# Six pairs of gate units per layer multiplied in seven quarter products (Strassen), placed behind the attention

## The chip, the cores and the metric

The kernel runs on one core of one Trainium2 chip. Five engines work side by side, each through its own queue of instructions: TensorE (PE) multiplies, VectorE (DVE), ScalarE (ACT) and GpSimd (POOL) compute on vectors, and SyncE (SP) issues the transfers. The metric is the time of one execution on the device in microseconds (us), the median of several runs.

## The reference, cut to what matters

Two layers of a decoder trunk with three attention branches a, b, c for 512 tokens and a model width of 1024. The part that the change touches is the merge. In short:

```
h = rmsnorm(x, norm_g[layer])                       # (512, 1024)
u = h @ w_in[layer]                                 # q, k, v, z of every branch, and ga, gb, gc: 3 x 1024 gate columns
ya, yb, yc = attention branches, each * silu(z)     # widths 256, 384, 384
merged = sigmoid(ga) * (ya @ w_br_a) + sigmoid(gb) * (yb @ w_br_b) + sigmoid(gc) * (yc @ w_br_c)
x = x + merged @ w_out[layer]
```

After the second layer a final RMSNorm follows. All is float32.

## The kernel before, in words

**Precision.** A float32 product is made of three matmuls in the type fp32r. Each operand is split into a high part (a cast to fp32r) and a low part (what the cast left); `mm3` (L125) adds high x high, high x low and low x high in PSUM.

**Tiling.** Everything is transposed: columns of a weight lie on the 128 partitions of the result and tokens run along its free dimension. A *unit* is 128 output columns for all 512 tokens: 8 k tiles of 128 input rows x 3 terms = 24 matmuls of 512 columns (`run_unit`, L133). The operands of the x side, XH[k] and XL[k], are x times norm_g, split, without the root of the mean square; that root, `rbc`, is multiplied in afterwards, at eviction.

**Weights.** They lie packed in `wpk` in the order of use, 256 KB per half a unit. `dma_to` (L880) issues their transfers on SP into five buffers called `raw`; `split_to` (L898) casts each on ACT (L905, `wh`) and subtracts on DVE (L907, `wl`). A ring of six such pairs, RING, runs ahead of PE.

**The M items.** `m_item(l, br, i)` (L570) makes one of the 24 gate units of a layer with its branch product: the unit (24 matmuls), then the product of the branch's result Y with its weights `p` (2 or 3 k tiles, 6 or 9 matmuls). What follows: L586 on DVE multiplies the gate by rbc out of PSUM, L587 on ACT takes tanh, L596 (L593 for branch 0) on DVE forms (tanh + 1) x product, and the result is added to the merge tile `mg`: by POOL for branch 1 (L598), by DVE for branch 2 (L600). After branch 2 the merge tile is complete and is split again: L605 on ACT casts, L606 on DVE subtracts. These split tiles, MH and ML, feed the output projection (`o_item`, L615, and in the last layer `last_projection`, which works in halves of 256 tokens).

**The order.** PE runs its instructions in the order in which the list `items` is written. That order is a hand-made plan: during the attention, 16 heads follow each other through scores, transposition and the product with v, and a dictionary `plan` puts projections (qa, kb, zc ...) and M items between them, so that PE has work while softmax runs on the other engines. There M(0,0..7) and M(1,0..7) are placed; M(2,0..7) follow behind the attention, one after another. On DVE, ACT and POOL the order comes from the Tile scheduler, which sorts by program order and priority; `urgent` (L111) raises the priority of what it wraps. PSUM has eight banks: three for units and branch products (`mm`), four for the attention (`att`), one `pv`. At the end of layer 1, from the last M item on, `manual_schedule` fixes the written order on all engines.

## Time and profile before

| | |
|---|---|
| time, median of 3 runs | 892.59 us (892.52 to 892.83) |
| the profiled execution | 892.23 us, of which the span of the core is 890.4 us |
| busy: PE | 879.3 us (99%), 4434 matmuls |
| busy: DVE | 607.4 us (68%), 1280 instructions |
| busy: ACT | 463.7 us (52%), 964 instructions |
| busy: POOL | 127.4 us (14%), 98 instructions |
| clock granted to PE | full (2.4 GHz) in all but the last of 40 slices, which shows 0.8 |
| transfers | 89.26 MB, mean 100 GB/s |

How to read it: busy time is an engine's own work within the span; several engines are busy at once. A matmul's duration is that of one instruction in a pipeline, so the time between two starts tells more than the duration of one. In time: the heads of layer 0 with their fillers run from about 60 to 338 us, M(2,0..7) from there to 399, then the output projection and the first projections of layer 1. In layer 1 the heads end at about 771 us and the last M item at 836; the last projection in halves closes the span.

### The profile page before, as it was taken

The numbers are of one execution on the slowest core, as the hardware profiler recorded it, in microseconds if no ns is written. First come the engines' busy times: TensorE is split into PE (matmuls) and PEld (weight loads), VectorE is DVE, ScalarE is ACT, GpSimd is POOL, SyncE is SP. The second block draws the span as 40 slices with busy tenths as digits, with TensorE's granted clock in tenths as the row PEclk, the third lists the DMA queues.
The fourth block names the chain that finished last, engine by engine and source line by source line (L and its number), as shares of the span: only waits on it lengthen the run. The fifth ranks groups of instructions, "written<-read, shape, count | busy, mean of one in ns | idle before, by whom it ended". The sixth has DMA issues, their size and how long they took to land.

```text
span 890.4 us, 13001 instructions
## 1 busy us (share of the span) xinstructions
PE 879.3 (99%) x4434; PEld 739.4 (83%) x4434; DVE 607.4 (68%) x1280; ACT 463.7 (52%) x964; POOL 127.4 (14%) x98
## 2 busy tenths in 40 slices
PE   9999999999999999999999999999999999999996
PEld 6988888888888888888889888888888888888895
DVE  7668899998765646554446879999886655555433
ACT  7467566665554434433335856666554544333542
POOL 5000231210001110001110012212100111100531
PEclk9999999999999999999999999999999999999998
DMA  6632322323232323335532332233222232233423
GB/s 216 187 96 71 107 72 89 113 69 94 73 98 82 95 84 105 95 98 167 149 134 84 85 86 85 77 101 101 83 84 76 87 89 86 77 98 94 129 78 113
DMA packets 53875, 89.26 MB, mean 100 GB/s; under 512 B 7344, under 2 KB 15920, under 8 KB 53808
## 3 DMA queue, kind: packets, MB, share of 16 engines
q1 hardware_dynamic: 53664, 88.42, 32.9%
q8 instruction: 35, 0.57, 0.3%
q14 instruction: 32, 0.26, 0.1%
q10 hardware_dynamic: 144, 0.01, 0.0%
HBM read 78.96 MB, written 4.19 MB: 93 GB/s over the span
## 4 chain that ended last, share of the span: by engine, by line
PE 96%; DVE 1%; issue 1%; DMA 1%; ACT 0%; SPq 0%; DVEq 0%; ACTq 0%
PE mm L127 26%; PE mm L128 26%; PE mm L126 26%; PE pv L545 4%; PE att L499 3%; PE att L435 2%; PE att L434 2%; PE att L230 1%; PE att L231 1%; PE att L229 1%; PE mm L256 1%; PE mm L257 1%; PE mm L258 1%; DMA mg<-in_xT_dram 1%; DVE xl L155 0%
## 5 line engine op out<-in xcount | busy, mean ns | idle before, releaser
L126 PE MATMUL mm<-xh,wh 128*128 128x512 f32 x736 | 293.1, 398 | 0.0
L905 ACT CAST wh<-raw 128x512 fp32r<-128x512 f32 (+3 forms) x277 | 163.4, 593 | 247.7 <-PE mm L127 191.7
L128 PE MATMUL mm<-xh,wl 128*128 128x512 f32 x736 | 290.5, 395 | 0.0
L127 PE MATMUL mm<-xl,wh 128*128 128x512 f32 x736 | 290.3, 394 | 0.0
L907 DVE TENSOR_TENSOR wl<-raw,wh 128x512 fp32r<-128x512 f32 (+3 forms) x272 | 182.4, 672 | 68.1 <-ACT wh L905 67.2
L128 PEld LDWEIGHTS mm<-xh,wl 128*128 128x128 f32 x736 | 138.2, 188 | 32.5
L127 PEld LDWEIGHTS mm<-xl,wh 128*128 128x128 f32 x736 | 138.4, 188 | 30.6
L126 PEld LDWEIGHTS mm<-xh,wh 128*128 128x128 f32 x736 | 138.4, 188 | 30.5
L470 ACT ACTIVATE P<-P,ng 128x256 f32<-128x256 f32 (+3 forms) x128 | 67.0, 525 | 38.0 <-DVE ng L468 38.0
L586 DVE TENSOR_TENSOR tmp<-mm,rbc 128x512 f32<-128x512 f32 x48 | 33.2, 691 | 55.9 <-PE mm L128 55.9
L345 POOL TENSOR_TENSOR tmp<-tmp,cos 128x512 f32<-128x512 f32 x20 | 31.4, 1568 | 257.8 <-DVE tmp L337 241.1
L127 PE MATMUL mm<-y,wh 128*128 128x512 f32 (+1 forms) x156 | 60.0, 384 | 0.3 <-DVE y L606 0.3
L126 PE MATMUL mm<-y,wh 128*128 128x512 f32 (+1 forms) x156 | 60.0, 384 | 0.0
L128 PE MATMUL mm<-y,wl 128*128 128x512 f32 (+1 forms) x156 | 60.0, 384 | 0.0
L598 POOL TENSOR_TENSOR mg<-mg,tmp 128x512 f32<-128x512 f32 x16 | 25.8, 1611 | 235.7 <-DVE tmp L596 235.7
L525 DVE TENSOR_TENSOR PL<-att,PH 128x512 fp32r<-128x512 f32 (+2 forms) x84 | 46.6, 600 | 0.2
L587 ACT ACTIVATE tmp<-tmp 128x512 f32<-128x512 f32 x48 | 30.4, 634 | 22.9 <-DVE tmp L586 22.8
L596 DVE SCALAR_TENSOR_TENSOR tmp<-tmp,mm 128x512 f32<-128x512 f32 x32 | 22.0, 688 | 28.5 <-PE mm L128 27.4
L524 ACT CAST PH<-att 128x512 fp32r<-128x512 f32 (+2 forms) x84 | 39.5, 526 | 2.4 <-PE att L499 1.2
L488 DVE TENSOR_SCALAR P<-P,den 128x256 f32<-128x256 f32 (+3 forms) x128 | 38.4, 364 | 1.1
L435 PE MATMUL att<-qk,qk 128*128 128x256 f32 (+2 forms) x128 | 37.1, 309 | 0.0
L499 PEld LDWEIGHTS att<-ident,P 128*128 128x128 f32 x284 | 32.9, 141 | 4.1
(197 smaller groups left out, 1374.5 us busy)
## 6 DMA issues: line engine op xcount, KB each, us to landing
raw<-in_wpk_dram SPq DMA_DIRECT2D x232, 256.0 KB, 2.6
raw<-in_wpk_dram SPq DMA_DIRECT2D x32, 192.0 KB, 2.3
tmp<-tmp SPq DMA_DIRECT2D x80, 64.0 KB, 2.0
raw<-in_wpk_dram SPq DMA_DIRECT2D x8, 260.0 KB, 2.8
mg<-in_xT_dram SPq DMA_DIRECT2D x8, 256.0 KB, 5.7
raw<-in_wpk_dram SPq DMA_DIRECT2D x16, 128.0 KB, 2.0
sz<-in_xT_dram SPq DMA_DIRECT2D x8, 256.0 KB, 3.0
x1d<-tmp SPq DMA_DIRECT2D x8, 256.0 KB, 3.3
```

The lines of the kernel that those rows point to most:

```text
L126: nc.tensor.matmul(ps, wh, xh, start=first, stop=False)
L127: nc.tensor.matmul(ps, wh, xl, start=False, stop=False)
L128: nc.tensor.matmul(ps, wl, xh, start=False, stop=last)
L435: nc.tensor.matmul(ps, q2[:, qs], k2[:, a:a + n], start=False, stop=True)
L470: nc.scalar.activation(pb, pb, AF.Exp, bias=ng[:, i:i + 1], scale=-1.0, accum_out=den[:, i:i + 1])
L488: nc.vector.tensor_scalar(blks[i], blks[i], den[:, i:i + 1], None, op0=ALU.mult)
L499: nc.tensor.transpose(ps[:, c * P:(c + 1) * P], pt[:, src * P:(src + 1) * P], st["ident"])
L524: nc.scalar.copy(hh, bk[:, :n])
L525: nc.vector.tensor_tensor(st["PL"][:, o:o + n], bk[:, :n], rd(hh), op=ALU.subtract)
L545: nc.tensor.matmul(ps[:, q:q + n], v[j], src[:, o:o + n], start=w == 0 and m == 0, stop=w == 1 and m == 3)
L905: (nc.vector.tensor_copy if i == 0 else nc.scalar.copy)(h[:, :w], r[:, :w])
L907: eng.tensor_tensor(lo[:, :w], r[:, :w], rd(h[:, :w]), op=ALU.subtract)
```

## The change

**What it does.** Per layer, M(0,0..7) and M(1,0..3) stay as they are. The other twelve M items become six pairs, (1,4), (1,6), (2,0), (2,2), (2,4) and (2,6): a pair is two neighbouring gate units, so 256 columns of a weight with 1024 rows, times 1024 x 512 of x. `pair_steps` multiplies each with Strassen's scheme in the form with seven products: weights and x are cut in 2 x 2 quarters, so a product multiplies 4 k tiles of 128 rows and 128 columns of weights with 256 tokens: 4 x 3 terms = 12 matmuls of 256 columns, and the seven take 84. Two M items took 2 x 24 = 48 matmuls of 512 columns for the same gates. The branch products of the pair stay (2 x 9 matmuls of 512 columns).

**Combinations of weights.** They are formed in place in the `raw` tiles before the split: form 2 on DVE (L1101), form 3 in two subtractions (L1103, L1104) and form 5 (L1106) on POOL. The four blocks B11, B12, B22, B21 of a pair are loaded ahead, and the `p` weights of pairs come through the two `sz` buffers.

**Combinations of x.** `sums(l, k)` forms once per layer, for each of the 4 k tiles, the four combinations that products 2 to 5 read: it loads the two x tiles, scales them on ACT, takes two halves on POOL and two on DVE (L601, L603), casts on ACT and subtracts the low part on DVE (L608). sums(3) is placed in the last head, sums(2), (0), (1) behind the attention, ahead of M(1,2) and M(1,3). The results lie in tiles that the attention no longer uses.

**Behind the products.** The seven products go into three PSUM banks a, b, c from the attention's pool, some added to what stands there. Evictions e1 (ACT, L728), c11 (DVE, L731), e5 (ACT, L735), e2 (ACT, L738), c12 (L741), c22 (L744) and c21 (L749, all DVE) bring the quarters together; L693 multiplies by rbc, L699 takes tanh, L706 forms the merge and L707 adds it on POOL for every pair but the last (2,6), where DVE adds. L718 and L719 split the finished merge of branch 2. All steps of branch 2 are `urgent`.

**Order.** The heads' slots b11 to b16 lose seven M items; M(1,2) and M(1,3) follow the attention, then the pairs. The output projection reads the k tiles in the order LATE, 7 before 6. The loader has new rules for when a buffer may be filled (`dma`).

In lines of the new kernel mm3 is at L127 to L129, the weights' transfer L1078, cast L1116 and subtraction L1118, M items' L629 (times rbc), L636 and L639 (merge), L641 (POOL's addition).

```diff
-MS = 7
+LATE = (0, 1, 2, 3, 4, 5, 7, 6)
...
+    def sum_places(k):
+        if k < 2:
+            return tuple(T([P, 8, P], F32R, f"vb{2 * k + w}").rearrange("p h d -> p (h d)") for w in range(2))
+        if k == 2:
+            return st["PH"][:, P:P + 1024], st["PL"][:, P:P + 1024]
+        return tuple(T([P, 1280], F32R, "P", 2)[:, :1024] for _ in range(2))
+
+    def sums_x(l, k):
+
+        src = xT if l == 0 else x1d
+        d = []
+        for kk in (k, k + 4):
+            t = tmp()
+            nc.sync.dma_start(t, src[:, kk, :])
+            nc.scalar.activation(t, t, AF.Copy, scale=g_sb[:, l, kk:kk + 1])
+            d.append(t)
+        return d
+
+    def sums(l, k):
+        def run():
+            a, b = sums_x(l, k)
+            u, v = tmp(), tmp()
+            nc.gpsimd.tensor_tensor(u[:, T0], a[:, T1], b[:, T1], op=ALU.add)
+            nc.vector.tensor_tensor(u[:, T1], u[:, T0], a[:, T0], op=ALU.subtract)
+            nc.gpsimd.tensor_tensor(v[:, T0], a[:, T0], a[:, T1], op=ALU.subtract)
+            nc.vector.tensor_tensor(v[:, T1], b[:, T0], u[:, T1], op=ALU.subtract)
+            h, lo = sum_places(k)
+            for n, w in ((0, u), (1, v)):
+                c = slice(n * S, n * S + S)
+                nc.scalar.copy(h[:, c], w)
+                nc.vector.tensor_tensor(lo[:, c], w, rd(h[:, c]), op=ALU.subtract)
+            st["SH", k], st["SL", k] = h, lo
+        return run
...
+    def pair_steps(l, br, i, last=False):
+
+        base = (0, 2, 5)[br]
+        n = NBR[br]
+        d = {}
+        now = urgent if br == 2 else (lambda fn: fn)
+
+        def A(half, tok):
+            return lambda k: (XH[k + 4 * half][:, tok], XL[k + 4 * half][:, tok])
+
+        def Sm(m):
+            c = slice((m - 1) * HT, m * HT)
+            return lambda k: (st["SH", k][:, c], st["SL", k][:, c])
+
+        def prod(bank, form, xf):
+            def pe(HL):
+                new = bank not in d
+                if new:
+                    d[bank] = att_bank()[:, :HT]
+                wh, wl = HL[0]
+                for k in range(4):
+                    c = slice(k * P, (k + 1) * P)
+                    xh, xl = xf(k)
+                    mm3(d[bank], wh[:, c], wl[:, c], xh, xl, new and k == 0, k == 3,
+                        bank != "c")
+            step(pe, [("w", l, br, i, form)])
+
+        def branch(u):
+            def pe(HL):
+                ps = d["p", u] = mm_bank()
+                wh, wl = HL[0]
+                for kk in range(n):
+                    yh, yo = st["Y", base + kk]
+                    mm3(ps, wh[:, kk * P:(kk + 1) * P], wl[:, kk * P:(kk + 1) * P], yh, yo,
+                        kk == 0, kk == n - 1)
+            step(pe, [("p", l, br, i + u)])
+
+        def norm(u, c):
+            def run():
+                gr = d["g", u][:, c]
+                nc.vector.tensor_tensor(gr, gr, st["rbc"][:, c], op=ALU.mult)
+            return run
+
+        def gate(u, c):
+            def run():
+                gr = d["g", u][:, c]
+                nc.scalar.activation(gr, gr, AF.Tanh, scale=0.5)
+            return run
+
+        def merge(u, c):
+            def run():
+                gr = d["g", u][:, c]
+                m = st["M", i + u][:, c]
+                nc.vector.scalar_tensor_tensor(gr, gr, 1.0, d["p", u][:, c], op0=ALU.add, op1=ALU.mult)
+                (nc.vector if last else nc.gpsimd).tensor_tensor(m, m, gr, op=ALU.add)
+                if br < 2:
+                    return
+                if ("MH", i + u, l) not in d:
+                    d["MH", i + u, l] = True
+                    pair = []
+                    for w in range(2):
+                        q = 2 * (i + u) + w
+                        pair.append(T([P, S], F32R, "qk", 12) if q < 12 else T([P, S], F32R, "y", 10))
+                    st["MH", i + u], st["ML", i + u] = pair
+                mh, ml = st["MH", i + u][:, c], st["ML", i + u][:, c]
+                nc.scalar.copy(mh, m)
+                nc.vector.tensor_tensor(ml, m, rd(mh), op=ALU.subtract)
+            return run
+
+        def start():
+            d["e"], d["e5"] = tmp(), tmp()
+            d["g", 0], d["g", 1] = tmp(), tmp()
+
+        def e1():
+            start()
+            nc.scalar.copy(d["e"][:, T0], d["a"])
+
+        def c11():
+            nc.vector.tensor_tensor(d["g", 0][:, T0], d["c"], d["e"][:, T0], op=ALU.add)
+            norm(0, T0)()
+
+        def e5():
+            nc.scalar.copy(d["e5"][:, T0], d["b"])
+
+        def e2():
+            nc.scalar.copy(d["e"][:, T1], d["a"])
+
+        def c12():
+            nc.vector.tensor_tensor(d["g", 1][:, T0], d["b"], d["e"][:, T1], op=ALU.add)
+
+        def c22():
+            nc.vector.tensor_tensor(d["g", 1][:, T1], d["a"], d["e5"][:, T0], op=ALU.add)
+            norm(1, slice(0, S))()
+            gate(1, slice(0, S))()
+
+        def c21():
+            nc.vector.tensor_tensor(d["g", 0][:, T1], d["a"], st["rbc"][:, T1], op=ALU.mult)
+            gate(0, T1 if last else slice(0, S))()
+
+        prod("a", 0, A(0, T0))
+        do(now(e1))
+        prod("c", 1, A(1, T0))
+        do(now(c11))
+        prod("b", 2, Sm(1))
+        do(now(e5))
+        prod("a", 3, Sm(2))
+        do(now(e2))
+        branch(0)
+        if last:
+            do(now(gate(0, T0)), now(merge(0, T0)))
+        prod("b", 4, Sm(4))
+        do(now(c12))
+        prod("a", 5, Sm(3))
+        do(now(c22))
+        branch(1)
+        do(now(merge(1, slice(0, S))))
+        prod("a", 6, A(1, T1))
+        do(now(c21))
+        do(now(merge(0, T1 if last else slice(0, S))))
+
 
...
+                if h == 16:
+                    do(sums(l, 3))
...
-        for i in range(8):
-            if l == 1 and i == MS:
+        for it in b_prev:
+            do(it[2], it[3])
+        for k in (2, 0, 1):
+            do(sums(l, k))
+        solo(M(1, 2))
+        solo(M(1, 3))
+        for br, i in ((1, 4), (1, 6), (2, 0), (2, 2), (2, 4), (2, 6)):
+            last = (br, i) == (2, 6)
+            if l == 1 and last:
                 do(lambda: ctx.enter_context(tc.manual_schedule()))
-            it = M(2, i)
-            step(it[1], it[0])
-            do(urgent(it[2]), urgent(it[3]))
+            pair_steps(l, br, i, last)
...
+
     seq = [c for it in items for c in it[0] or ()]
-    raw, hl = {}, {}
+    loads, at = [], {}
+    for i, key in enumerate(seq):
+        if key[0] == "w":
+            _, l, br, u, form = key
+            if form == 0:
+                c = [COL["g" + "abc"[br]] + P * (u + w) for w in range(2)]
+                for name, blk, last in (("B11", ("u", l, c[0], 0), 3), ("B12", ("u", l, c[1], 0), 6),
+                                        ("B22", ("u", l, c[1], 1), 6), ("B21", ("u", l, c[0], 1), 8)):
+                    loads.append(dict(name=(key[:4], name), blk=blk, tag="raw", last=i + last, since=0))
+        else:
+            pair = i > 0 and key[0] == "p" and any(k[:3] == ("w", key[1], key[2]) and k[3] in (key[3], key[3] - 1)
...
+    def source(key):
+
+        if key[0] != "w":
+            return raw.pop(key)
+        form = key[4]
+        b11, b12, b21, b22 = (raw[key[:4], n][:, :S] for n in ("B11", "B12", "B21", "B22"))
+        if form == 2:
+            nc.vector.tensor_tensor(b11, b12, b11, op=ALU.subtract)
+        if form == 3:
+            nc.gpsimd.tensor_tensor(b11, b22, b11, op=ALU.subtract)
+            nc.gpsimd.tensor_tensor(b21, b21, b11, op=ALU.subtract)
+        if form == 5:
+            nc.gpsimd.tensor_tensor(b12, b22, b12, op=ALU.subtract)
+        return (b11, b21, b11, b11, b22, b12, b21)[form]
+
     def split_to(n):
         while ptr["split"] < min(n, len(seq)):
             i = ptr["split"]
-            w = off[seq[i]][1]
-            h, lo = places(seq[i])
-            r = raw.pop(i)
+            key = seq[i]
+            w = S if key[0] == "w" else off[key][1]
+            r = source(key)
+            h, lo = places(key)
             (nc.vector.tensor_copy if i == 0 else nc.scalar.copy)(h[:, :w], r[:, :w])
-            eng = nc.gpsimd if seq[i][:2] == ("o", L - 1) else nc.vector
...
```

In the plan the lines of slots b11 to b16 read now: b11 none, a12 (0, 6), a13 zc 1, a14 zc 2, a15 (0, 7), a16 (1, 0), b16 (1, 1), the others none.

**Where the order changes, first place: DVE between the attention's end and the first gate evictions.** wl is the low part of a weight, tmp a gate or a sum of x, PL and vb the low parts of the sums. Before, in branch 1, a gate's operations (L586, L596) and weights' low parts (L907) by turns:

```order
L907 TENSOR_TENSOR wl_3380<-raw_3294,wh_3379 128x512
L586 TENSOR_TENSOR tmp_3395<-mm_3335,rbc_560 128x512
L907 TENSOR_TENSOR wl_3384<-raw_3296,wh_3383 128x512
L596 SCALAR_TENSOR_TENSOR tmp_3395<-tmp_3395,mm_3360 128x512
L907 TENSOR_TENSOR wl_3388<-raw_3298,wh_3387 128x384
L557 TENSOR_TENSOR ys_3400<-pv_3370,tmp_3398 64x512
L907 TENSOR_TENSOR wl_3451<-raw_3317,wh_3450 128x512
L586 TENSOR_TENSOR tmp_3470<-mm_3406,rbc_560 128x512
L907 TENSOR_TENSOR wl_3455<-raw_3333,wh_3454 128x512
L596 SCALAR_TENSOR_TENSOR tmp_3470<-tmp_3470,mm_3431 128x512
L907 TENSOR_TENSOR wl_3459<-raw_3391,wh_3458 128x384
```


Now:

```order
L1118 TENSOR_TENSOR wl_3348<-raw_3147,wh_3347 128x512
L608 TENSOR_TENSOR PL_131<-tmp_3210,PH_130 128x512
L608 TENSOR_TENSOR PL_131<-tmp_3211,PH_130 128x512
L1101 TENSOR_TENSOR raw_3147<-raw_3162,raw_3147 128x512
L1118 TENSOR_TENSOR wl_3352<-raw_3305,wh_3351 128x512
L601 TENSOR_TENSOR tmp_3226<-tmp_3226,tmp_3220 128x256
L603 TENSOR_TENSOR tmp_3227<-tmp_3223,tmp_3226 128x256
L1118 TENSOR_TENSOR wl_3357<-raw_3147,wh_3356 128x512
L608 TENSOR_TENSOR vb_721_3233<-tmp_3226,vb_720_3232 128x512
L608 TENSOR_TENSOR vb_721_3233<-tmp_3227,vb_720_3232 128x512
L1118 TENSOR_TENSOR wl_3387<-raw_3147,wh_3386 128x512
L629 TENSOR_TENSOR tmp_3307<-mm_3256,rbc_560 128x512
```


The eviction L629 of M(1,2)'s gate stands behind the low parts of sums(2) and sums(0) (L608), form 2 (L1101) and four weights; before, between a gate's eviction and the operation ahead of it in the queue stood one or two weights.

**Second place: DVE in the middle of branch 2.** Before, the tail of one M item and the start of the next (L596 merge, L600 addition, L606 split of the result):

```order
L586 TENSOR_TENSOR tmp_3587<-mm_3552,rbc_560 128x512
L907 TENSOR_TENSOR wl_3636<-raw_3475,wh_3635 128x512
L596 SCALAR_TENSOR_TENSOR tmp_3587<-tmp_3587,mm_3577 128x512
L907 TENSOR_TENSOR wl_3640<-raw_3533,wh_3639 128x384
L600 TENSOR_TENSOR mg_1719<-mg_1719,tmp_3587 128x512
L606 TENSOR_TENSOR qk_3593<-mg_1719,qk_3592 128x512
L907 TENSOR_TENSOR wl_3694<-raw_3535,wh_3693 128x512
```


Now, the second half of the pair (2,2), with product 0's weights of (2,4) in the last row:

```order
L741 TENSOR_TENSOR tmp_3945<-att_3971,tmp_3942 128x256
L1118 TENSOR_TENSOR wl_4057<-raw_3838,wh_4056 128x512
L744 TENSOR_TENSOR tmp_3945<-att_3925,tmp_3943 128x256
L693 TENSOR_TENSOR tmp_3945<-tmp_3945,rbc_560 128x512
L1118 TENSOR_TENSOR wl_4076<-raw_3838,wh_4075 128x512
L706 SCALAR_TENSOR_TENSOR tmp_3945<-tmp_3945,mm_4063 128x512
L1118 TENSOR_TENSOR wl_4100<-sz_4020,wh_4099 128x384
L749 TENSOR_TENSOR tmp_3944<-att_3925,rbc_560 128x256
L719 TENSOR_TENSOR qk_4082<-mg_2400,qk_4081 128x512
L1118 TENSOR_TENSOR wl_4125<-raw_3965,wh_4124 128x512
```


A split of a finished merge (L719) stands between the last quarter's eviction (L749) and the next weights, as L606 did before L907; it now reads what POOL wrote.

**Same place on ACT.** Before:

```order
L587 ACTIVATE tmp_3587<-tmp_3587 128x512
L905 CAST wh_3639<-raw_3533 128x384
L605 CAST qk_3592<-mg_1719 128x512
L905 CAST wh_3693<-raw_3535 128x512
L905 CAST wh_3697<-raw_3550 128x512
```


Now:

```order
L1116 CAST wh_4075<-raw_3838 128x512
L699 ACTIVATE tmp_3945<-tmp_3945 128x512
L1116 CAST wh_4099<-sz_4020 128x384
L718 CAST qk_4081<-mg_2400 128x512
L1116 CAST wh_4124<-raw_3965 128x512
```


The cast L718 of the finished merge stands ahead of the cast of the next product's weights, as L605 did.

**Same place on POOL.** Before, POOL has nothing in branch 2; the last rows are branch 1's additions, and the next is the following stage:

```order
L598 TENSOR_TENSOR mg_2500<-mg_2500,tmp_3252 128x512
L598 TENSOR_TENSOR mg_2657<-mg_2657,tmp_3395 128x512
L598 TENSOR_TENSOR mg_2729<-mg_2729,tmp_3470 128x512
L598 TENSOR_TENSOR mg_2821<-mg_2821,tmp_3537 128x512
L166 TENSOR_TENSOR ys_4084<-ys_4084,tmp_4132 128x512
```


Now, the pair (2,2) whole:

```order
L1106 TENSOR_TENSOR raw_3899<-raw_3965,raw_3899 128x512
L1103 TENSOR_TENSOR raw_3838<-raw_3965,raw_3838 128x512
L1104 TENSOR_TENSOR raw_3969<-raw_3969,raw_3838 128x512
L707 TENSOR_TENSOR mg_2400<-mg_2400,tmp_3945 128x512
L707 TENSOR_TENSOR mg_2071<-mg_2071,tmp_3944 128x512
```


Five operations of POOL per pair stand where none stood: form 5, form 3 in two, and the additions for both units.

## Rows read from the trace of the kernel before

**Rows 1.** The page's parts 1 and 2: busy time and share; the granted clock.
```profile
PE 879.3 (99%) x4434; PEld 739.4 (83%) x4434; DVE 607.4 (68%) x1280; ACT 463.7 (52%) x964; POOL 127.4 (14%) x98
...
PEclk9999999999999999999999999999999999999998
```

**Rows 2.** The page's part 4, chain that ended last, share by engine.
```profile
PE 96%; DVE 1%; issue 1%; DMA 1%; ACT 0%; SPq 0%; DVEq 0%; ACTq 0%
```

**Rows 3.** The chain in order of time, 780 to 800: start, us, what.
```profile
780.13 0.23 PE mm L126
...
799.89 0.23 PE mm L127
```

**Rows 4.** The same chain in the last projection, 836 to 850.
```profile
836.51 0.12 PE mm L126
...
849.99 0.12 PE mm L126
```

**Rows 5.** Windows: stretch, length, then PE, PEld, DVE, ACT, POOL, clock, DMA share, GB/s.
```profile
345.00:399.00 54.00, 54.00 (x234) 43.67 (x234) 31.49 (x51) 21.29 (x35) 0.00 (x0) 1.00 0.34 99
```

**Rows 6.** Timeline: start, duration, engine, line, operation; paces of DVE and ACT.
```profile
105.12 0.69 DVE L565 TENSOR_TENSOR y<-ys,y 128x512 fp32r<-128x512 f32 x1
...
105.72 0.69 DVE L907 TENSOR_TENSOR wl<-raw,wh 128x512 fp32r<-128x512 f32 x1
...
166.87 0.42 DVE L907 TENSOR_TENSOR wl<-raw,wh 128x256 fp32r<-128x256 f32 x1
...
167.21 0.69 DVE L565 TENSOR_TENSOR y<-ys,y 128x512 fp32r<-128x512 f32 x1
...
835.13 1.66 ACT L905 CAST wh<-raw 128x512 fp32r<-128x512 f32 x3
```

**Rows 7.** Timeline: POOL and DVE operations that overlap, at three places.
```profile
272.52 0.68 DVE L907 TENSOR_TENSOR wl<-raw,wh 128x512 fp32r<-128x512 f32 x1
...
272.68 1.68 POOL L598 TENSOR_TENSOR mg<-mg,tmp 128x512 f32<-128x512 f32 x1 [6.88 <-DVE tmp L596]
...
273.54 0.68 DVE L557 TENSOR_TENSOR ys<-pv,tmp 64x512 f32<-64x512 f32 x1
...
825.92 1.29 POOL L907 TENSOR_TENSOR wl<-raw,wh 128x512 fp32r<-128x512 f32 x1 [0.76 <-ACT wh L905]
...
826.21 1.56 DVE L600 TENSOR_TENSOR mg<-mg,tmp 128x512 f32<-128x512 f32 x1
...
833.88 0.69 DVE L600 TENSOR_TENSOR mg<-mg,tmp 128x512 f32<-128x512 f32 x1
```

**Rows 8.** Groups by line and shape: 256 columns on POOL and on ACT.
```profile
L695 POOL TENSOR_TENSOR tmp<-mg,rbc 128x256 f32<-128x256 f32 x4 | 2.9, 734 | 30.2 <-ACT rbc L687 30.2
...
L687 ACT COPY rbc<-pv 128x256 f32<-128x256 f32 x2 | 0.7, 363 | 1.7 <-PE pv L213 1.7
```

**Rows 9.** The page's part 6: size and time to landing of a weight's transfer.
```profile
raw<-in_wpk_dram SPq DMA_DIRECT2D x232, 256.0 KB, 2.6
```

**Rows 10.** Windows, as in rows 5, over three heads late in the attention.
```profile
263.40:286.90 23.50, 23.50 (x115) 19.49 (x114) 12.81 (x30) 9.77 (x23) 4.90 (x3) 1.00 0.31 88
```

**Rows 11.** The chain in order of time at the last merge, 832 to 837.
```profile
833.16 0.70 DVE tmp L596
...
833.88 0.70 DVE mg L600
...
834.61 0.63 ACT y L605
...
835.26 0.70 DVE y L606
...
836.00 0.39 PE mm L127
```

More of the change, by code (lines that the diff above doesn't have):

```diff
@@ L561, in rest @@
             nc.vector.tensor_tensor(ys, ys, st["sz", pair], op=ALU.mult)
-            yh = T([P, S], F32R, "y", 10)
-            yo = T([P, S], F32R, "y", 10)
+            if pair < 6:
+                yh, yo = T([P, S], F32R, "y", 10), T([P, S], F32R, "y", 10)
+            else:
+                yh, yo = (T([P, S], F32R, f"va{2 * pair - 12 + w}") for w in range(2))
             nc.scalar.copy(yh, ys)
@@ L567, in pv_item @@
         return pe, copy, plus, rest if o else None
+    HT = S // 2
+    T0, T1 = slice(0, HT), slice(HT, S)
+    def sum_places(k):
[28 more added lines that the diff above has]
+        return run
     def m_item(l, br, i):
@@ L621, in pe @@
                 load_res(1)
-            d["ps"] = run_unit(HL, [st["MH", i] for i in range(8)], [st["ML", i] for i in range(8)])
+            d["ps"] = run_unit(HL, [st["MH", i] for i in range(8)], [st["ML", i] for i in range(8)], LATE)
         def post():
@@ L655, in pe @@
             ps = mm_bank()[:, :HT]
-            for k in range(KT):
+            for k in LATE:
                 wh, wl = st["WO", e][k // 4]
@@ L919, in tile_trunk @@
         nc.sync.dma_start(xs[k], xT[:, k, :])
-        dma_to(min(k + 1, RAW))
+        dma(0, min(k + 1, RAW))
     split_x(xs[0], 0, 0, 2)
@@ L947, in tile_trunk @@
         split_to(pos + len(chunks))
-        dma_to(ptr["split"] + RAW)
+        dma()
         fn([hl.pop(i) for i in range(pos, pos + len(chunks))])
@@ L959, in tile_trunk @@
         split_to(pos + RING)
-        dma_to(ptr["split"] + RAW - 1)
+        dma(1)
         pos += len(chunks)
```

65 lines of the change are left out of this document (40 added, 25 removed).

## The prediction

> **What bounds the kernel now.** I read the page's first two parts first: TensorE (PE) is busy for 99% of the span and its clock is granted in full in every slice; VectorE (DVE) has 68%, GpSimd (POOL) 14% [rows 1]. Busy PE is not yet bound PE, so the chain of waits comes next: 96% of it is PE [rows 2]. In the stretch that the change rewrites the chain is nothing but matmuls at an even pace: from 780.13 to 799.89 there are 85 steps of 0.2325 us with 512 columns [rows 3], and in the last projection, from 836.51 to 849.99, 114 steps of 0.1182 us with 256 columns [rows 4]. PE is the bound, and a 256-column matmul, each with its own weights, costs 0.51 of a 512-column one. Beside it, in 345 to 399, DVE is busy for 58% and POOL not at all [rows 5]; this spare time is what the change spends.
>
> **What it removes on PE.** Two gate units are 48 matmuls of 512 columns, 48 x 0.2325 = 11.16 us; seven products of four k tiles and three terms are 84 of 256 columns, 84 x 0.1182 = 9.93 us. A pair saves 1.23 us, the 12 pairs 14.7 us. With its two branch products (18 x 0.2325 = 4.18) a pair takes 14.11 us of PE, where two M items took 15.34.
>
> **What it adds beside PE.** First the paces. DVE starts a 512-wide operation every 0.60 us and a 256-wide one every 0.34; ACT starts casts every 0.52 to 0.55 [rows 6]. POOL needs 1.29 us for 512 columns that nothing disturbs [rows 7] and 0.73 for 256; a 256-wide copy on ACT alone takes 0.36 [rows 8], and some 0.31 in a row. In a pair DVE has seven lo parts of weights, two of branch weights (0.47), form 2, four evacuations, two norms and two merges: 7 x 0.60 + 0.94 + 0.60 + 4 x 0.34 + 0.94 + 1.20 = 9.2 us; pairs of branch 2 add two lo parts of the merged result, 10.4. POOL has three form subtractions and two additions, 6.5 us. Against 14.11 either fits. They don't fit side by side. L600, an addition of two SBUF tensors, started 0.29 us into a POOL subtraction and took 1.56 us, ending 0.56 after POOL; L598 on POOL, started 0.16 after a DVE subtraction, took 1.68 and ended 1.16 after it; L557, which reads PSUM, took its usual 0.68 beside POOL [rows 7]. Whichever of the two starts first keeps the other out, if DVE reads two SBUF tensors.
>
> The Trainium skill says the same as a rule that speaks against this change: "SBUF — State Buffer", section "Who interferes with whom", calls the port pair that VectorE and GpSimd share an exclusive lock and not a split of bandwidth. By that rule the sum is the one below; if the two only shared bandwidth it would be the first rival's. The trace agrees, with the 1.56 against 0.69 us.
>
> So each POOL piece between two such DVE operations costs DVE 1.16 + 0.55 = 1.71 us instead of 0.60. I follow the queues as the order shows them.
>
> **A pair of branch 0 or 1.** From the end of POOL's last addition, DVE's queue: p1 weights 0.47, norm 0.34, two weights 1.20, form 2 0.60, weights 0.69, [form 5 on POOL 1.16], weights 0.55, [form 3, first half 1.34], norm 0.55, [second half 1.16], weights 0.47, merge 0.60, p weights 0.55, [addition 1.16], weights 0.46, merge 0.60, weights 0.69, [addition 1.16] = 13.75 us. The evacuations from PSUM pass beside POOL. Under 14.11: PE stays the bound.
>
> **A pair of branch 2.** Here the lo parts and casts of the finished merge (L719, L718) stand in DVE's and ACT's queues ahead of the next weights, and each waits for POOL's addition. The same round: four ACT steps until product 0's weights are cast (0.56 + 0.53 + 0.31 + 0.65), DVE 0.60 + form 2 0.60 + weights 0.69, form 5 1.16, weights 0.55, form 3 1.34, norm 0.55, second half 1.16, weights 0.47, merge 0.60, p weights 0.55, addition 1.16, cast 0.67, four DVE steps 0.60 + 0.60 + 0.60 + 0.69, addition 1.16 = 15.8 us. That is a closed ring without PE, and longer than 14.11. From the pair (2,0) to (2,6) there are three such turns; the first is partly covered, since e1 is needed only 2.8 us after its product and c21 1.4 us after (I find 0.6 lost of 1.7). Given back per layer: 0.6 + 1.7 + 1.7 = 4.0. B21 of the next pair is loaded only when product 5's weights are split; its 2.6 us [rows 9] behind another load may be late by 0.5 a turn, so I take 4.5, between 0.8 (all POOL work beside PSUM work) and 6.
>
> **The stretch before the pairs.** The sums of x (4 k tiles, 8 half additions on POOL, 4 x 1.88 us on DVE) lie beside M(1,1) to M(1,3). In DVE's queue the evacuation of M(1,2)'s gate (L629), which frees the bank for M(1,3)'s branch product, now stands behind sums(2), sums(0), form 2 and the weights of products 0 to 3. From the start of M(1,1): on SP the x tiles of sums(2) stand behind a weight load that waits until 4.2; three loads land by 9.0; scaled on ACT 9.7; two POOL halves 11.1; differences, weights, two lo parts 13.6; form 2 and weights 14.9; form 5 16.1; POOL halves of sums(0) 17.5; differences 18.2; weights 18.8, lo 19.4; form 3 20.6, lo 21.1, second half 22.3; weights 22.9; L629 23.5. The branch product could start at 7.67 + 7.67 + 5.58 = 20.9. PE waits 2.5 us (0 to 3.5). DVE leaves this 1.3 us late, and in (1,4) e1 and c21 hold PE for 0.35 + 1.1 (0 to 2).
>
> **At no cost.** The attention loses seven M items as filler around its last heads. In 263.4 to 286.9 DVE was busy for 12.8 us with two M and a z item [rows 10]; less 2 x 2.9 and 2.4 for these, a head has 4.6, and with a z item 7.0 in the 8.2 us that PE now has per head; what T needs of the softmax is finished some 3 us ahead. 0, at worst 2 in all; if this cover fails the band heads wait for DVE. The turned order of k (LATE) covers unit 6: after the last product 18 matmuls of 512 columns run (4.2 us) before unit 7 is read. In layer 1 they have 256 (2.1 us), and six splits of W_out on POOL lie among the last merges, but the old end lost little too: the chain L596, L600, L605, L606 ended 0.04 us before PE went on [rows 11], about 0.4 us of waiting. Net 0.3 (-0.4 to 1.5).
>
> **The sum.** Per layer 4.5 + 2.5 + 1.45 = 8.45 us are given back, 16.9 in both, and 0.3: 17.2 against 14.7. The profiled execution took 892.23 (span 890.4 and 1.8 around it), so 894.7; it lies 0.36 under the median of the three runs, so the forecast is 895.0 us: **a little slower**.
>
> **The rivals.** *PE keeps the bound.* If DVE's PSUM operations fall beside POOL's and the queues run ahead, a branch 2 pair costs its port time at least: POOL 6.5 + DVE's SBUF operations 7.9 = 14.4 us, 0.3 over PE. With 0.8 per layer there, 0.5 before the pairs and 0.3 after, 3.2 in all, the time is 892.6 - 14.7 + 3.2 = 881; this decides if DVE's weights are cast before POOL asks for the port. For it: DVE has 26% of a pair free. Against: the same queue carries what PE waits for and what waits for POOL. *Half of it:* the turn of a branch 2 pair stays near 15.0 or the stretch before the pairs hides: 886 to 891. *The ring is longer still:* if every hand-over adds 0.05 us to some 20 steps and the late load another 0.5, a turn is 17.3, three turns lose 3 us more per layer, and 895 becomes 900. *The change doesn't do what it says:* a 256-column product costs more than half, since PE loads weights twice as often; rows 4 are that case already, so I give it nothing.
>
> **How the numbers follow.** A measurement of this kernel can tell some 0.2% (1.8 us) from no change. The main case has 0.55, with 890 to 898 as its own range: slower than 894.4 in 0.30 of it, within in 0.20, faster in 0.05. PE keeping the bound 0.17 and half of it 0.18 (0.14 faster, 0.04 within); the longer ring 0.10, slower. Together: faster 0.36, same 0.24, slower 0.40. The range leaves out one in ten on either side: 882 to 900.
>
> **What would show it.** Right: from (2,0) on the pairs stand 15.5 to 16.3 us apart, branch 1 pairs near 14.2; L719 and the weights after it wait for POOL's L707, PE's product 1 for DVE's L749 and product 3 for ACT's L728; DVE's weight subtractions rise from 0.69 towards 1 us; M(1,3)'s branch product waits 2 to 3 us for L629. Wrong: if all pairs stand 14.1 to 14.4 apart, the port sum failed; if PE waits inside the attention, the cover there did; if it waits before product 2, the sums came too late.

## The result

The changed kernel takes **905.27 us** (median of 4 runs, 904.64 to 905.80), the kernel before beside it 892.56: a ratio of 1.0142, 95% interval 1.0125 to 1.0160. It is slower by 12.7 us, where 2.4 were forecast with 900 as the upper end of the range. The span of the profiled execution grew from 890.4 to 904.0 us, by 13.5.

The profile after, the lines of the page that answer to [rows 1, 2]: busy time by engine, the granted clock, the chain by engine.

```profile
PE 871.9 (96%) x4866; PEld 754.7 (83%) x4866; DVE 706.2 (78%) x1402; ACT 508.0 (56%) x1072; POOL 212.4 (24%) x162
...
PEclk9999999999999899999999999999999998999998
...
PE 78%; issue 7%; DVE 5%; POOL 4%; ACT 3%; DMA 2%; SPq 0%; POOLq 0%; DVEq 0%; ACTq 0%
```

PE now holds 78% of the chain instead of 96%, and DVE, POOL and ACT have taken shares: PE waits. Its clock has two slices with an 8 that were not there. PE's busy time fell by 7.4 us only, though its work fell by 14.7 us.

What PE waits for, in us over the whole span, with the number of waits and the longest:

```profile
PE mm L127 <- DVE tmp L629: 12.0, 2, 6.0
PE att L127 <- ACT tmp L728: 7.0, 6, 1.5
...
PE mm L127 <- ACT y L718: 0.7, 1, 0.7
```

So there are two places: once per layer the branch product of M(1,3) waits for the eviction L629, 6.0 us long, and three times per layer product 3 of a pair waits for e1 (L728) to leave bank a. Around the first of these waits, the windows of the changed kernel (columns as in [rows 5]) and the chain in order of time:

```profile
300.00:310.00 10.00, 4.68 (x21) 3.41 (x19) 7.88 (x11) 5.14 (x9) 6.97 (x6) 0.96 0.17 52
310.00:320.00 10.00, 9.37 (x50) 8.53 (x51) 9.62 (x14) 5.41 (x10) 4.12 (x4) 0.70 0.23 74
```

```profile
306.02 1.65 POOL raw L1103
...
307.70 0.63 ACT wh L1116
...
308.35 1.53 DVE wl L1118
309.88 0.61 DVE tmp L629
310.50 0.14 issue
310.63 0.77 PE mm L127
311.40 0.43 PE mm L128
...
314.38 0.43 PE mm L129
314.81 0.21 PE att L127
...
316.09 0.12 PE att L127
...
321.07 0.23 PE mm L127
```

Straight ahead of L629 the chain holds half of a form 3 on POOL (L1103), the cast of its result, and a weight subtraction on DVE that took 1.53 us instead of 0.69.

A clock of 0.96 and 0.70 as the mean of 10 us, with the lower level at one half, makes 0.8 + 6.0 = 6.8 us at half clock (1.2 GHz). The first 0.8 lie ahead of 310.00, while PE still stood; the chain shows the others: after the wait 512 columns take 0.43 us instead of 0.23 and 256 take 0.21 instead of 0.12, until 316.09. Nine matmuls of 512 and six of 256 columns took 316.09 - 310.63 = 5.46 us, at full pace 9 x 0.2325 + 6 x 0.1182 = 2.80: **the wait cost another 2.7 us per layer through the clock.**

The account of the 13.5 us, both layers together, beside the terms of the prediction (waits of PE are counted from start to start of two matmuls, less the pace of one; the lists of waits above give somewhat less):

| | forecast | measured |
|---|---|---|
| less work on PE | -14.7 | -14.7 (worked out from the paces) |
| wait for L629 ahead of the pairs | +5.0 | +12.3 (6.1 and 6.2) |
| half clock after it | not in the sum | +5.3 (2 x 2.7) |
| pair (1,4), e1 and c21 | +2.9 | 0 |
| pairs of branch 2 | +9.0 | +8.0 (0.9, 1.7, 1.7 and 0.9, 1.7, 1.2) |
| end of layer 1 | +0.3 | +1.9 |
| attention without its fillers | 0 | +0.7 |
| sum | +2.5 | +13.5 |

(The attention's row: seven M items of 33 matmuls, 7 x 33 x 0.2325 = 53.7 us, left it; the time from its first scores to its last product with v fell by 53.2 us in layer 0 and 53.5 in layer 1.)

### The profile page after: what moved, and what is told of

It reads as the page before. It is cut to its first block, busy times and chain, and to the rows that moved or that the text cites. A ratio compares the mean times of both kernels' runs of the same rounds, so it can differ in the third digit from the quotient of the medians.

```text
span 904.0 us, 14292 instructions
## 1 busy us (share of the span) xinstructions
PE 871.9 (96%) x4866; PEld 754.7 (83%) x4866; DVE 706.2 (78%) x1402; ACT 508.0 (56%) x1072; POOL 212.4 (24%) x162
## 4 chain that ended last, share of the span: by engine, by line
PE 78%; issue 7%; DVE 5%; POOL 4%; ACT 3%; DMA 2%; SPq 0%; POOLq 0%; DVEq 0%; ACTq 0%
PE mm L127 18%; PE mm L128 17%; PE mm L129 17%; PE pv L546 4%; PE att L500 3%; PE att L127 3%; PE att L128 3%; PE att L129 3%; PE att L436 2%; PE att L435 2%; DVE wl L1118 2%; ACT wh L1116 1%; PE att L231 1%; PE att L232 1%; PE att L230 1%
## 5 line engine op out<-in xcount | busy, mean ns | idle before, releaser
L1116 ACT CAST wh<-raw 128x512 fp32r<-128x512 f32 (+3 forms) x289 | 172.9, 602 | 191.8 <-PE mm L128 105.4
L1118 DVE TENSOR_TENSOR wl<-raw,wh 128x512 fp32r<-128x512 f32 (+3 forms) x284 | 214.8, 759 | 50.6 <-ACT wh L1116 48.0
L127 PE MATMUL mm<-xh,wh 128*128 128x512 f32 x544 | 217.5, 400 | 0.0
L129 PE MATMUL mm<-xh,wl 128*128 128x512 f32 x544 | 214.8, 395 | 0.0
L128 PE MATMUL mm<-xl,wh 128*128 128x512 f32 x544 | 214.6, 395 | 0.0
L129 PEld LDWEIGHTS mm<-xh,wl 128*128 128x128 f32 x544 | 102.1, 188 | 24.0
L128 PEld LDWEIGHTS mm<-xl,wh 128*128 128x128 f32 x544 | 102.3, 188 | 22.5
L127 PEld LDWEIGHTS mm<-xh,wh 128*128 128x128 f32 x544 | 102.3, 188 | 22.4
L127 PE MATMUL mm<-y,wh 128*128 128x512 f32 (+1 forms) x124 | 49.1, 396 | 12.7 <-DVE tmp L629 12.0
L129 PE MATMUL mm<-y,wl 128*128 128x512 f32 (+1 forms) x124 | 48.8, 394 | 0.0
L600 POOL TENSOR_TENSOR tmp<-tmp,tmp 128x256 f32<-128x256 f32 x8 | 6.8, 844 | 149.6 <-ACT tmp L592 149.6
L127 PE MATMUL att<-xh,wh 128*128 128x256 f32 x144 | 41.0, 284 | 0.0
L128 PE MATMUL att<-xl,wh 128*128 128x256 f32 x144 | 40.9, 284 | 0.0
L129 PE MATMUL att<-xh,wl 128*128 128x256 f32 x144 | 40.9, 284 | 0.0
L707 POOL TENSOR_TENSOR mg<-mg,tmp 128x512 f32<-128x512 f32 x20 | 32.2, 1610 | 33.1 <-DVE tmp L706 33.1
L127 PEld LDWEIGHTS mm<-y,wh 128*128 128x128 f32 x124 | 24.1, 194 | 17.6 <-issue 12.8
```

The lines of the kernel that those rows point to most:

```text
L127: nc.tensor.matmul(ps, wh, xh, start=first, stop=False, skip_group_check=part)
L128: nc.tensor.matmul(ps, wh, xl, start=False, stop=False, skip_group_check=part)
L129: nc.tensor.matmul(ps, wl, xh, start=False, stop=last, skip_group_check=part)
L707: (nc.vector if last else nc.gpsimd).tensor_tensor(m, m, gr, op=ALU.add)
L1116: (nc.vector.tensor_copy if i == 0 else nc.scalar.copy)(h[:, :w], r[:, :w])
L1118: eng.tensor_tensor(lo[:, :w], r[:, :w], rd(h[:, :w]), op=ALU.subtract)
```

## The experiments

Two theories stood after the result. One: DVE and POOL keep each other out, so that POOL's help in the pairs and in the sums of x makes both the ring of 15.9 us and most of the wait ahead of the pairs. The other: the stretch ahead of the pairs is late because of its order, L629's place in DVE's queue or the late loads of x, or because DVE simply has too much to do. All ratios are to the kernel before in the same job (892.05 to 892.22 us).

**e1, the M item written between the sums.** PE's order stays; L629 of M(1,2) stands ahead of sums(0).

```diff
-        for k in (2, 0, 1):
-            do(sums(l, k))
+        do(sums(l, 2))
         solo(M(1, 2))
+        do(sums(l, 0), sums(l, 1))
         solo(M(1, 3))
```

> The M item (1,2) is written between sums(2) and sums(0) instead of behind all three sums; PE's order is the same, its gate's eviction L629 now stands on VectorE ahead of sums(0). Theory (the 6.1 us in which TensorE stands before M(1,3)'s branch product are made by the place of L629 in VectorE's queue behind sums that wait for x): the wait falls to under 1 us in both layers and no 6.8 us at half clock follow, 8.8 us less per layer; but pair (1,4) comes earlier by that, and its product 2 then waits 4 to 4.6 us for sums(1), which end no earlier: 896 to 897 us, or 902 if that wait brings the half clock too. Rival (VectorE simply has too much work there, so that the place in the queue doesn't matter): TensorE's waits in the stretch together stay at 6 us, 903 to 906.

904.70 us, ratio 1.0138 (1.0123 to 1.0153). PE's waits in e1:

```profile
PE att L127 <- ACT vb L607: 7.6, 4, 3.1
PE att L127 <- ACT tmp L728: 7.4, 6, 1.5
PE att L128 <- DVE vb L608: 2.0, 4, 0.7
```

The wait for L629 is gone, and 9.6 us of waits for the sums' parts (L607, L608) of k = 0 and 1 stand in its place, all in product 2 of pair (1,4): from start to start 6.4 us in layer 0 and 5.3 in layer 1, against 6.1 and 6.2. The half clock came again, 6.8 us per layer. The place in the queue decided only where PE waits. That is what the rival forecast, in the waits (6 us) and in the time (903 to 906). Of the theory only the new place of the wait came true; neither 896 to 897 nor 902 with the half clock did.

**e2, the x tiles of sums(2) loaded one item earlier**, ahead of M(1,1):

```diff
+            if h == 16:
+                x2 = []
+                do(lambda: x2.extend(sums_x(l, 2)))
             for n, it in enumerate(B):
                 step(it[1], it[0])
...
-            a, b = sums_x(l, k)
+            a, b = d or sums_x(l, k)
```

> The two x tiles of sums(2) are loaded and scaled one item earlier, ahead of M(1,1) instead of behind it. Theory (sums(2) start late because their loads stand on SyncE behind a weight load that waits for a free buffer until 290.8 us of the span): loads go 5 us earlier or more, sums(2) end 3 to 5 us earlier, the wait for L629 falls from 6.1 to 1 to 2.5 us, and the half clock goes with it: 889 to 893 us. Rival (the ports of VectorE and GpSimd or VectorE's load set the end of the sums): L629 moves by less than 1 us, 903 to 905.

899.94 us, 1.0081 (1.0064 to 1.0097): between the two. In the changed kernel the loads (SP's queue), the weight ahead of them and what followed were these lines of the timelines (M(1,1) starts at 283.61):

```profile
290.12 0.68 DVE L1118 TENSOR_TENSOR wl<-raw,wh 128x512 fp32r<-128x512 f32 x1
...
290.83 0.33 SPq L1078 DMA_DIRECT2D raw<-in_wpk_dram  x1
291.25 0.86 SPq L591 DMA_DIRECT2D tmp<-in_xT_dram  x2
...
296.74 0.74 POOL L600 TENSOR_TENSOR tmp<-tmp,tmp 128x256 f32<-128x256 f32 x1 [2.26 <-ACT tmp L592]
...
309.81 0.68 DVE L629 TENSOR_TENSOR tmp<-mm,rbc 128x512 f32<-128x512 f32 x1
```

In e2, whose lines from L1007 on lie three further down, so that form 3 is L1106 and L1107 and a weight's subtraction L1121 (timelines of SP, DVE, POOL and ACT, then the first of PE's waits):

```profile
286.12 0.90 SPq L591 DMA_DIRECT2D tmp<-in_xT_dram  x2
...
303.33 0.68 DVE L629 TENSOR_TENSOR tmp<-mm,rbc 128x512 f32<-128x512 f32 x1
...
306.94 1.41 POOL L1106 TENSOR_TENSOR raw<-raw,raw 128x512 f32<-128x512 f32 x1 [0.97 <-DVE wl L1121]
...
307.12 1.78 DVE L608 TENSOR_TENSOR vb<-tmp,vb 128x512 fp32r<-128x512 f32 x1
...
310.01 1.73 POOL L641 TENSOR_TENSOR mg<-mg,tmp 128x512 f32<-128x512 f32 x1
...
310.53 1.76 DVE L1121 TENSOR_TENSOR wl<-raw,wh 128x512 fp32r<-128x512 f32 x1
...
314.67 0.37 ACT L728 COPY tmp<-att 128x256 f32<-128x256 f32 x1
```

```profile
PE att L127 <- ACT tmp L728: 14.1, 8, 4.2
```

The loads went out 5.1 us earlier and L629 ran 6.5 us earlier, early enough that PE doesn't wait for it. Not all of this is the loads: with them the scheduler also set L629 ahead of form 3 (L1106 at 306.94, L629 at 303.33), where the changed kernel has it behind the form's first half and that half's weight subtraction (306.02 and 308.35 in the chain above). The same holds for e5 and e8. Then two of DVE's subtractions started inside POOL's form 3 and POOL's addition L641 and took 1.78 and 1.76 us instead of 0.69, and e1 of pair (1,4) came so late that PE stood 4.2 us ahead of product 3. The late loads were a link of the chain; the next one, POOL and DVE, was hardly shorter.

**e3 and e9, PE kept busy in the waits.** e3 puts 18 matmuls into an unused bank ahead of M(1,3)'s branch product, e9 another 10 ahead of product 3 of (1,4). They compute nothing that is used.

```diff
             d["g"] = run_unit(HL, XH, XL)
+            if (br, i) == (1, 3):
+                spare = att_bank()
+                for n in range(18):
+                    nc.tensor.matmul(spare, HL[0][0][:, :P], XH[n % KT], start=True, stop=True)
...
+                if (br, i, form) == (1, 4, 3):
+                    spare = att_bank()
+                    for n in range(10):
+                        nc.tensor.matmul(spare, wh[:, :P], XH[n % KT], start=True, stop=True)
```

> 18 matmuls of 512 columns that write an unused bank (4.2 us at full clock) stand on TensorE between M(1,3)'s gate unit and its branch product; nothing else is changed by hand, though VectorE's order then has three weights instead of four ahead of L629 (1.5 us). Theory (TensorE's clock falls to half because of the 6 us in which it stands, and this costs 2.7 us per layer beside the wait): no stretch at 0.5 in either layer, time 905.3 less 2 x (2.7 + 1.5) = 897; with the wait unchanged 900. Rival (the clock falls for another reason, the 256-column products for one): the half clock stays, 902 to 905.

905.15 us, 1.0143 (1.0128 to 1.0158): a miss, and it decided nothing by itself. The wait at L629 was filled in layer 0, a wait of 2.1 us ahead of product 3 came up behind it, and half a clock followed that one, as the window of those 10 us in e3 shows (0.88 on the mean); so e9 filled it too.

```profile
310.00:320.00 10.00, 8.05 (x54) 7.44 (x53) 9.44 (x15) 5.91 (x13) 3.35 (x2) 0.88 0.33 90
```

> As e3, with 10 more matmuls of 512 columns into an unused bank (2.3 us) ahead of product 3 of pair (1,4), where TensorE stood for 2.1 and 2.3 us in e3 and its clock then was half for 3.4 us in each layer. The waits are the same, only TensorE is busy in them. Theory (the half clock follows TensorE's standing): no stretch at half clock in layer 0, in layer 1 at most one, since 1.4 us are still left open there; time below e3's 905.1 by 1.7 to 3.4, so 901.7 to 903.4. Rival (the half clock comes from the stretch's work, not from the waits): both stretches stay, 905 to 907.

903.74 us, 1.0130 (1.0113 to 1.0147), a span of 901.9 against e3's 904.3. The same window in e9:

```profile
310.00:320.00 10.00, 10.00 (x68) 9.11 (x67) 9.33 (x15) 6.28 (x13) 3.36 (x2) 1.00 0.28 76
```

The clock is full in e9, in layer 1 as well, with DVE, ACT and POOL working as in e3. The half clock follows PE's standing, not the stretch's work. It is the clock that decides this: the time lies 0.3 us above the theory's range, and the intervals of e3 and e9 overlap.

**e4, POOL left out of the pairs.** Forms 3 and 5 and the additions to the merge run on DVE.

```diff
-            nc.gpsimd.tensor_tensor(b11, b22, b11, op=ALU.subtract)
-            nc.gpsimd.tensor_tensor(b21, b21, b11, op=ALU.subtract)
+            nc.vector.tensor_tensor(b11, b22, b11, op=ALU.subtract)
+            nc.vector.tensor_tensor(b21, b21, b11, op=ALU.subtract)
...
-            nc.gpsimd.tensor_tensor(b12, b22, b12, op=ALU.subtract)
+            nc.vector.tensor_tensor(b12, b22, b12, op=ALU.subtract)
...
-                (nc.vector if last else nc.gpsimd).tensor_tensor(m, m, gr, op=ALU.add)
+                nc.vector.tensor_tensor(m, m, gr, op=ALU.add)
```

> Forms 3 and 5 and the additions to the merge run on VectorE instead of GpSimd, so GpSimd has nothing left in the pairs. Theory (the ring of 15.9 us per pair of branch 2 is made of hand-overs between VectorE and GpSimd, which keep each other out, and of the split that waits for GpSimd): VectorE has 13.4 us of work per pair, under TensorE's 14.1, the pairs of branch 2 stand 14.1 to 14.3 apart and the stalls of 8.0 us in all fall under 1.5; time 905.3 less 7 = 898, the stretch before the pairs about as before. Rival (VectorE's load itself sets the pace, it is busy for 96% there): the turn grows from 15.9 to over 17 us and the time to 908 or more.

891.45 us, 0.9991 (0.9981 to 1.0000): 13.8 us less than the changed kernel, twice what was expected. The waits for L728 are gone from PE's list altogether, and what is left of the other is

```profile
PE mm L127 <- DVE tmp L629: 7.4, 2, 3.9
```

The ring went as expected. The rest came from terms that the expectation left alone: form 5 and form 3 stand ahead of L629 and no longer hold DVE there (L629 starts 24.2 us after M(1,1) instead of 26.2, with the loads as late as before), and the end of layer 1 lost most of its waits.

**e6 and e7, each half of e4 alone**: e6 moves the forms, e7 the additions.

> Only forms 3 and 5 run on VectorE; GpSimd keeps the additions to the merge. Theory (every GpSimd operation between VectorE's keeps it out): the ring of 15.9 us loses 1.16 + 1.34 + 1.16 us and gains 3 x 0.60 us, so 14.0, just under TensorE's 14.1: the pairs of branch 2 stand 14.1 to 14.5 apart, stalls fall from 8.0 us to under 2; the wait for L629 falls as in e4 (by 2 us): 892 to 895. Rival (the link from GpSimd's addition to the split and on to the next weights makes the ring, whatever the forms do): stalls stay at 6 us or more, 897 to 900.

> Only the additions to the merge run on VectorE; GpSimd keeps forms 3 and 5. Theory (every GpSimd operation between VectorE's keeps it out): the ring loses twice 1.16 us and gains twice 0.60, 15.9 to 14.7 us; stalls fall from 8.0 to 2 to 4 us, the stretch before the pairs stays: 899 to 902. Rival (the link from GpSimd's addition to the split makes the ring): the stalls vanish altogether, 896 to 898.

e6: 891.47 us, 0.9990 (0.9981 to 1.0000), 0.5 under the theory's range and far from the rival's. e7: 897.02 us, 1.0052 (1.0037 to 1.0067), in the rival's range (896 to 898) and not in the theory's (899 to 902). The profile of e7 is that of its fastest run, 895.08. The turn of the ring is read from e1 to e1, L728 on ACT's timeline in layer 0. In the changed kernel:

```profile
362.21 0.36 ACT L728 COPY tmp<-att 128x256 f32<-128x256 f32 x1
378.11 0.36 ACT L728 COPY tmp<-att 128x256 f32<-128x256 f32 x1
393.99 0.36 ACT L728 COPY tmp<-att 128x256 f32<-128x256 f32 x1
```

In e6:

```profile
356.67 0.36 ACT L728 COPY tmp<-att 128x256 f32<-128x256 f32 x1
371.40 0.36 ACT L728 COPY tmp<-att 128x256 f32<-128x256 f32 x1
```

In e7:

```profile
372.88 0.35 ACT L728 COPY tmp<-att 128x256 f32<-128x256 f32 x1
387.50 0.35 ACT L728 COPY tmp<-att 128x256 f32<-128x256 f32 x1
```

In e4:

```profile
357.42 0.37 ACT L728 COPY tmp<-att 128x256 f32<-128x256 f32 x1
371.50 0.36 ACT L728 COPY tmp<-att 128x256 f32<-128x256 f32 x1
```

15.9 us a turn in the changed kernel; 14.7 with the forms on DVE (expected 14.0); 14.6 with the additions on DVE (expected 14.7); 14.1 with both, PE's own pace. In e6 and e7 a turn is still over 14.1, but three turns don't last long enough for the lateness of e1 to reach PE: stalls of 0.3 us in all in e6 and of 0.4 us per layer in e7 are left, fewer than the 2 to 4 that were expected of e7. Either kind of POOL work makes the ring about as much longer. That it is the link from POOL's addition to the split alone, as the rival says whose time e7 met, is ruled out by e6, where that link stands unchanged and the stalls are gone all the same.

**e5, e8 and e10: POOL out of the sums too, with and without the earlier loads.** e5 is e4 with e2; e8 is e5 with the sums' halves on DVE; e10 is e8 without the earlier loads.

```diff
-            nc.gpsimd.tensor_tensor(u[:, T0], a[:, T1], b[:, T1], op=ALU.add)
+            nc.vector.tensor_tensor(u[:, T0], a[:, T1], b[:, T1], op=ALU.add)
...
-            nc.gpsimd.tensor_tensor(v[:, T0], a[:, T0], a[:, T1], op=ALU.subtract)
+            nc.vector.tensor_tensor(v[:, T0], a[:, T0], a[:, T1], op=ALU.subtract)
```

> Forms and additions on VectorE as in e4, and the x tiles of sums(2) loaded one item earlier as in e2. Theory (two separate causes: hand-overs between VectorE and GpSimd in the pairs, and late loads of x ahead of them; the half clock follows a wait of some 3 us or more): the waits of 4.1 and 3.6 us for L629 that e4 still has go, and the half clock with them; what takes their place ahead of product 3 (4.3 us in e2, where GpSimd's forms held VectorE) is at most 2 us: 878 to 884. Rival (VectorE is so full between the attention and the pairs that the wait only moves on, as in e1): a wait of 3 us or more ahead of product 3 in both layers and the half clock stays, 888 to 892.

885.85 us, 0.9926 (0.9911 to 0.9941). L629's wait is gone, 2.9 and 2.3 us ahead of product 3 are left, and one half clock of 3.4 us in layer 0: just short of what was expected, and away from the rival.

> As e5, and the eight halves that the sums of x take on GpSimd run on VectorE too (0.34 us each instead of 0.74 and two hand-overs). Theory (VectorE and GpSimd keep each other out, so GpSimd's help is none): the sums end 1 to 2 us earlier, waits ahead of the pairs under 1 us per layer, no half clock: 877 to 881. Rival (VectorE's load is what binds in this stretch): the waits grow by the 2.7 us that VectorE gets, 883 to 890.

**879.28 us, 0.9855 (0.9840 to 0.9870)**: faster than both kernels, and as expected. The first of PE's waits is one at the start of the program, none is left in the pairs or ahead of them, and the clock is full in every slice but the last, as before. Head of the list of waits, then two lines of the page:

```profile
PE pv L1131 <- DVE qk L1128: 1.5, 1, 1.5
```

```profile
PE 864.9 (99%) x4866; PEld 750.8 (86%) x4866; DVE 700.5 (80%) x1474; ACT 510.4 (58%) x1072; POOL 114.3 (13%) x90
...
PEclk9999999999999999999999999999999999999998
```

The row of busy times is the plainest evidence that the two engines hold each other up: DVE does 72 instructions more than in the changed kernel (1474 against 1402) and is busy for 5.7 us **less** (700.5 against 706.2), and POOL, which lost those 72, is busy for 98 us less. The span is 877.1, so 13.3 of the 14.7 us that PE saves have arrived.

> As e8 without the earlier loads: forms, additions and the sums' halves on VectorE, the x tiles of sums(2) loaded behind the weight load as in the changed kernel. Theory (the loads are a cause of their own): sums(2) start 3 to 5 us later than in e8 and TensorE waits 1.5 to 4 us per layer ahead of the pairs: 883 to 889. Rival (without hand-overs to GpSimd the late loads are hidden): no wait over 0.5 us, 879 to 881.

880.64 us, 0.9870 (0.9856 to 0.9885), with 1.7 us of waiting for L629 in both layers together: the rival's time, but not its condition (no wait over 0.5 us). The run doesn't leave the loads where the changed kernel has them. Here they are, with M(1,1) starting at 282.67:

```profile
287.74 0.90 SPq L591 DMA_DIRECT2D tmp<-in_xT_dram  x2
```

They went out 5.1 us after M(1,1)'s start, in the changed kernel 7.6, since DVE was done earlier with the subtraction that frees the buffer. And the scheduler moved eight matmuls of product 0 of (1,4), 0.95 us, ahead of M(1,3)'s branch product; in no other experiment is the order of PE's products another than in the changed kernel. So the 1.4 us between e8 and e10 are not the price of the late loads, and the intervals of the two overlap. With POOL still in the sums the earlier loads, and the order that came with them, were worth 5.6 us (e4 to e5). What e10 does show is that taking POOL out of the pairs and the sums, with nothing else changed by hand, gives back 24.6 us (905.27 to 880.64).

## Why the prediction was wrong

**What held.** PE's saving is 14.7 us (12 x 1.231 is 14.8): without stalls the turn is 14.1 us (e4), forecast 14.11. The ring of a branch 2 pair was forecast at 15.8 and stands at 15.9, link by link. From the timelines of DVE, POOL and ACT at one turn, and PE's product 3:

```profile
371.58 1.64 POOL L1104 TENSOR_TENSOR raw<-raw,raw 128x512 f32<-128x512 f32 x1
...
372.19 1.57 DVE L1118 TENSOR_TENSOR wl<-raw,wh 128x512 fp32r<-128x512 f32 x1
...
373.69 0.67 DVE L706 SCALAR_TENSOR_TENSOR tmp<-tmp,mm 128x512 f32<-128x512 f32 x1
...
374.29 0.55 DVE L1118 TENSOR_TENSOR wl<-sz,wh 128x384 fp32r<-128x384 f32 x1
...
374.44 1.54 POOL L707 TENSOR_TENSOR mg<-mg,tmp 128x512 f32<-128x512 f32 x1 [1.22 <-DVE tmp L706]
...
376.02 0.62 ACT L718 CAST qk<-mg 128x512 fp32r<-128x512 f32 x1 [2.89 <-POOL mg L707]
...
376.55 0.61 ACT L1116 CAST wh<-raw 128x512 fp32r<-128x512 f32 x1
...
378.11 0.36 ACT L728 COPY tmp<-att 128x256 f32<-128x256 f32 x1
...
378.52 0.38 PE L127 MATMUL att<-vb,wh 128*128 128x256 f32 x1 [1.55 <-ACT tmp L728]
```

POOL's L707 starts 0.15 us into a subtraction of DVE (374.29) and ends 1.1 after it; the cast L718 waits for it with the next weights behind it; e1 comes four ACT steps later, and PE waits for e1. The subtraction at 372.19 takes 1.57 us beside POOL's form, where [rows 7] had 1.56. This is the exclusive lock that the Trainium skill ("SBUF — State Buffer", section "Who interferes with whom") states, and this case's traces agree with it. e4 to e8 show what it costs: with more instructions on DVE (1422 to 1474 against 1402), DVE was busy for 698.3 to 706.0 us, never for longer than in the changed kernel (706.2).

**The step that failed: the stretch ahead of the pairs,** 2.5 us a layer in the sum, with 3.5 as its upper bound, and 8.8 measured (6.1 of waiting and 2.7 of half clock). Three things in it:

- *The start of the sums.* The prediction put the x loads of sums(2) behind a weight load that waits until 4.2 us after M(1,1)'s start (283.61). That load waited for a buffer that the subtraction at 290.12 frees, and went out at 290.83, 7.2 after the start. DVE stood there behind the gating of the attention's last head. From then on the forecast chain is right, late by 3.4 to 3.6 us at each link: POOL's second half done at 14.6 instead of 11.1, L629 done at 26.9 instead of 23.5. So the wait of 2.5 us became 6.1. A queue was followed through one engine (SP) but not through the one that releases it (DVE).
- *The clock.* No term and no rival had it. The trace of before never let PE stand in the middle of the program, so its clock was full in all slices but the last (the prediction says in every slice); what a wait of some microseconds does to the clock was left out. It made 5.3 us.
- *What a bound is.* The upper bound of 3.5 us came from varying the steps, not from asking what happens if one of them moves. e1 and e2 show why that is too narrow: the sums, forms and evictions are one chain, and when one link is cured the wait turns up at the next, so the whole chain's length was the term: with POOL in it 6 us over, without it and with the earlier loads (e8) nothing, without it alone (e10) some 2 us, half of them covered by the matmuls that moved.

**Terms that came out smaller or larger.** Pair (1,4) cost nothing instead of 1.45 us a layer; the longer wait ahead of it had let DVE catch up, and in e2, where that wait is gone, (1,4) does wait. The end cost 1.9 instead of 0.3. One half is a wait of 0.96 us for a split of W_out on POOL (L1118), which the kernel before doesn't have and every run here has, with 0.8 to 1.0. The other is the waits for the last merge (L718, L719): 1.5 us in the changed kernel, 1.4 with the forms on DVE (e6), 1.0 with the additions there (e7), 0.3 with both (e4), against some 0.5 before. The attention lost 0.7, inside the bound of 2.

**The rivals.** "PE keeps the bound" at 881 was given 0.17 with a condition: that DVE's work falls clear of POOL's. The changed kernel doesn't meet it, e8 does by taking POOL out, at 879. The longer ring, with 900, had the direction right and the place wrong. By its own figures (17.3 against 15.8, three turns a layer) it loses 4.5 us more per layer, not 3, which makes 904; had it been put so, it would have come near the measured time by luck, for the ring stood at 15.9.

**What stays open.** What the late loads alone cost: with the earlier loads of e2, e5 and e8 L629 changed its place in DVE's queue, and e10, meant to keep the loads late, has them earlier than the changed kernel. With the additions on DVE (e7) PE still stands 5.3 and 6.1 us ahead of the pairs, with the forms there (e6) 4.4 and 4.5; that fits the queue, where the forms stand ahead of L629 and the additions behind it, but it wasn't tested further. In layer 0 of e7 the loads went out 0.9 us earlier than in the changed kernel.

## What to carry to other kernels

An operation given to GpSimd is relief for VectorE where VectorE's neighbouring operations read PSUM. Between additions and subtractions of two SBUF tensors it can cost VectorE more time than the operation itself would: by [rows 6, 7] a neighbour that takes 0.60 us then takes 1.71, so 1.1 us more, where the operation on VectorE would add 0.60. (This is an estimate for a piece that meets such neighbours; over all 72 pieces of e8 VectorE gained 5.7 us.) Follow a late transfer back to the instruction that frees its buffer, on whatever engine that stands, before writing down when it starts. And where a forecast lets TensorE stand for some microseconds, add what the clock takes after it, as a term of its own.
